# Encoder layer with dense expert products: where the transposes of two gate builds stand among blocks of U, and where the first G is loaded

## The chip, the cores and the metric

The kernel runs on one core of a Trainium2 chip. The metric is the device time of one execution in microseconds (us), lower is better. The engines are TensorE (PE; PEld is its weight load), VectorE (DVE), ScalarE (ACT), GpSimd (POOL) and SyncE (SP). SP, ACT and POOL also issue DMA transfers; rows of SPq or ACTq are such issues.

## What is computed

One post-norm encoder layer on 512 tokens of width 1024: layer norm, a combined in-projection, neighbourhood attention and latent attention, an output projection, a layer norm, then a mixture of 16384 experts with one row of U and one of V each, a gate, and the last layer norm. The experts are what the change touches:

```python
def one_chunk(xb):                                  # 128 tokens
    q = (xb @ w_q).reshape(128, 8, 256)
    s1 = jnp.einsum('thd,kd->thk', q[..., :128], sub_keys[0])
    s2 = jnp.einsum('thd,kd->thk', q[..., 128:], sub_keys[1])
    v1, i1 = lax.top_k(s1, 16)
    v2, i2 = lax.top_k(s2, 16)
    ...
    cv, ci = lax.top_k(cand, 16)                    # 16 of 256 sums
    e1 = jnp.take_along_axis(i1, ci // 16, axis=-1)
    e2 = jnp.take_along_axis(i2, ci % 16, axis=-1)
    idx = (e1 * 128 + e2).reshape(128, 8 * 16)      # 128 experts a token
    g = jax.nn.softmax(cv, axis=-1).reshape(128, -1)
    hpre = jnp.einsum('td,ted->te', xb, u_table[idx])
    act = g * jax.nn.gelu(hpre, approximate=False)
    return jnp.einsum('te,ted->td', act, v_table[idx])
```

## The kernel before

The 512 tokens are four chunks of 128. For chunk 0 the rows of U and V that its tokens chose are gathered. Chunk 1 (`NGC`) takes its U products from gathered rows ("own rows") and V densely. Chunks 2 and 3 are dense in both: all 16384 rows of U are multiplied, and a matrix G, mostly zeros, holds each token's gate weight for each expert. The gates make the dense result equal to the sparse one.

**The blocks of U.** U comes in blocks of 512 KB (tile `raw` or `raw_u`), loaded by SP (L1251) as buffers come free. `lead_block` multiplies a block with the 256 dense tokens (`whole`) in eight products of 128x256 (L1291) into a PSUM tile, "mm" or, in the stage `gating` at the end, one of two "hp" buffers. ACT applies the Gelu (`ge`, L1273); the first 96 results are sent to `ge_dram` on ACT's queue (L1275). 108 blocks (LEAD) are multiplied ahead of the loop. `run_pe(amount)` hands out products of U one by one until an account, `due`, is used up: so the written order on each engine is fixed when the program is built, and a constant such as `LAG` or `WAIT` is an amount of U products to put at a place.

**A build of G** (`build_g`) begins with three transposes on PE (L1090: the two expert indices and the weights, `e1`, `e2`, `gw`). DVE and ACT cast them out of PSUM (`eT` and `ne`, L1098, L1101, L1102, L1103, L1104). Then come 16 sets: DVE and ACT write one-hot rows (`oh_i`, L1144, L1148, L1149; `oh_j`, L1156), PE multiplies 16 pairs of them (L1115, into two PSUM tiles "tr"), and ACT copies the result to `g_st` (L1128). After four sets a quarter of G is complete and is sent to `g_dram` in four parts on ACT's queue (L1073); `send` issues one part, and `run` calls it once per step. The builds are those of chunk 2, chunk 3 ("the second build") and chunk 1 ("the last build").

**Rows.** POOL gathers one row of U per token (L1174) into five buffers in turn (`whi`, `wlo`, `row`, `whi`, `wlo`), DVE takes its product with the token (L1176, into `s_dot` for own rows, `hdot` for chunk 0). The own rows go beside the second build, 26 rows of chunk 0 (`beside`) beside the last. Near the end of these, at row 14 of 26, `SEAM` puts a lot of U products off, so that two sets of the last build follow each other with none between.

**The loop's first G.** The loop over 128 expert blocks that follows (L1551, `acc`; V blocks as `v_raw`, L1489) reads G in groups of eight blocks (tile `gt`, L1474). The first group, `first_g`, is loaded from `g_dram` early (L1447), but the quarters of chunk 1 are copied into it from `g_st`.

**Where the order is set.** All this stands in one written order for the five engines. What the words below call "ahead of" is a place in that order on one engine; semaphores make the engines wait for each other. Each DMA issue of SP and ACT takes the next of eight completion semaphores in turn, and so waits for the DMA eight issues back.

Of the kernel before, what the change touches and what calls it, by code (L numbers as in the profile page):

```python
# [31 lines left out]
N_S = 128  # L32
N_U = N_D - N_S
GT = 32
G_PARTS = 4
GB = 8
LEAD = 108
SPILL = 96
# [2 lines left out]
FIRST = 40  # L41
PACE = 1.1
AHEAD = 14.0
LAG = 6.0
BESIDE = 26
PRE = BESIDE
OWN = 1.2
OWN_G = 0.7
OWN_G_LATE = 4.0
SEAM = 7.0  # L50
WAIT = 8.4
OWN_LATE = 10.0
LATE = 0.57
OT = 8
# [25 lines left out]
def tile_encoder_layer(ctx: ExitStack, tc: tile.TileContext, A: dict, out: bass.AP):  # L80
    nc = tc.nc
# [214 lines left out]
    with tc.tile_pool(name="ln0", bufs=1, reuse_waits="tile") as ln0, \  # L296
# [122 lines left out]
        parts = turn(0)  # L419
# [17 lines left out]
        parts = turn(1)  # L437
# [8 lines left out]
        parts = turn(2)  # L446
# [8 lines left out]
        parts = turn(3)  # L455
# [374 lines left out]
    NGC, NDC = N_G // 128, N_D // 128  # L830
# [3 lines left out]
    g_dram = dram.tile([NTG, 128, 128 * GT], F32, name="g_dram")  # L834
# [107 lines left out]
    for g in range(16):  # L942
# [8 lines left out]
        if g:  # L951
            i, t = next(homes)
# [113 lines left out]
    parts = []  # L1066

    def send():

        if parts:  # L1070
            g, t, x = parts.pop(0)
            n = 128 // G_PARTS
            nc.scalar.dma_start(g_dram[g][:, x * n * GT:(x + 1) * n * GT],  # L1073
                                t[:, x * n:(x + 1) * n].rearrange("p i t -> p (i t)"))

    def run_pe(amount):
        nonlocal due
        due += amount * PACE
        while due > 0:
            done = next(pe_work, 1e9)  # L1080
            due -= done
        if due < -1e6:
            due = 0.0

    def build_g(c, e1, e2, gw):
# [55 lines left out]
        for q in range(128 // OT):  # L1141
            oh = bt.tile(wide, F16, name="oh_i")
            by_v = [128, 2 * np_ - OI_ACT, 128, 2]
            nc.vector.tensor_tensor(oh[:, OI_ACT:], pairs.unsqueeze(1).to_broadcast(by_v),  # L1144
                                    keys[:, q].rearrange("p s (a b) -> p (s a) b", b=2)[:, OI_ACT:].unsqueeze(2)
                                    .to_broadcast(by_v), op=OP.is_equal)
            for i in range(2 * OI_ACT):
                nc.scalar.activation(oh[:, i // 2, :, i % 2], iota, AF.Abs, bias=ne[:, OT * q + i:OT * q + i + 1])  # L1148
            nc.scalar.activation(oh[:, 0:OI_ACT], oh[:, 0:OI_ACT], AF.Relu, bias=1.0, scale=-1.0)  # L1149
            if ahead:  # L1150
                sums = products(*ahead)
                due -= G_SPLIT
            yield SPLIT_OH
            oj = bt.tile([128, 2, np_, 128, 2], F16, name="oh_j")
            for part in range(2):
                nc.vector.tensor_tensor(oj[:, part], oh[:, np_:],  # L1156
                                        wt[:, q, part].rearrange("p (a b) -> p a b", b=2).unsqueeze(2)
                                        .to_broadcast([128, np_, 128, 2]), op=OP.mult)
                if part == 0:
                    yield SPLIT_OJ  # L1160
            if ahead:
                leave(ahead[0], sums)
            ahead = (q, oh, oj)
            yield SPLIT_OJ
# [93 lines left out]
    def fill():  # L1258
        while loaded < LEAD and load_u():
            pass  # L1260
# [158 lines left out]
    with tc.manual_schedule(engines={nc.vector.engine, nc.scalar.engine, nc.tensor.engine, nc.sync.engine,  # L1419
                                     nc.gpsimd.engine}):  # L1420
        fill()
        held = []
        run(route(NGC, held))
        own = own_rows(*held)
        run_pe(next(own))
        own_due = -OWN_LATE
        for c in range(NGC + 1, 4):
            res = []
            if c > NGC + 1:
                run(route(0, []), OWN)  # L1430
            run(route(c, res), OWN)
            if c > NGC + 1:
                run_pe(WAIT)
            run(build_g(c, *res), OWN)
        own_due = 1e9
        run([0.0], 1.0)
        side = beside()
        run_pe(next(side))
        for _ in own:
            pass  # L1440
        own = None
        run_pe(LAG)

        while parts:
            send()
        first_g = pX.tile([128, NTG, GB, GT], F32, name="gt1")
        nc.sync.dma_start(first_g[:, 128 // GT:].rearrange("p g i t -> p g (i t)"),  # L1447
                          g_dram[128 // GT:, :, SPILL * GT:(SPILL + GB) * GT].rearrange("g p x -> p g x"))
        build = build_g(NGC, *held)
        next(build)  # L1450
        run_pe(next(side))
        own = side
        own_due = -OWN_G_LATE
        run(build, OWN_G)
        for x in own:
            run_pe(x)
        while parts:
            send()
        pb.close()
# [103 lines left out]
    with tc.manual_schedule(engines={nc.vector.engine, nc.sync.engine}):  # L1563
        for n, i in enumerate(order):
# [38 lines left out]
            parts = [t.rearrange("p (g t) -> p g t", t=GT) for t in (ah, al)] + [a]  # L1603
            if n in v_cut:
                held_a.append([t[:, :N_S // GT] for t in parts])
                parts = [t[:, N_S // GT:] for t in parts]
# [131 lines left out]
```

## Time and profile before

| | |
|---|---|
| time, median of 3 runs | 1490.76 us (1490.73 to 1491.14) |
| the profiled execution | 1489.54 us, span 1487.8 us |
| the second and the last build with the U blocks beside them | about 700 to 893 us |
| second build's transposes, last build's transposes | just ahead of DVE's casts at 712.32 and 810.35 us |
| last gate product, end of U, start of the loop | 878.27, 893.29, 893.29 us |
| the loop over expert blocks | 893 to about 1440 us |

All times in rows are microseconds from the start of the span. A row of the timeline has start, duration, engine, line, operation, out<-in, the shape, the count, and in brackets the idle time ahead of it with what released it. A row of a view of windows has the window, its length, the busy time of PE, PEld, DVE, ACT and POOL, the granted clock of TensorE (1.00 is full speed), the mean busy share of the DMA engines and GB/s. A row of the waits has the engine and line that waited, the one that it waited for, us in total, times, and the longest.

### The profile page before, as it was taken

Reading aid. Unit: us, or ns where it says so; the run is one execution under the profiler, and the core shown is the slowest. Engines: PE = TensorE matmul, PEld = TensorE weight load, DVE = VectorE, ACT = ScalarE, POOL = GpSimd, SP = SyncE. Lnnn points to the kernel's source line nnn. Section 1 sums busy time; section 2 is a strip of 40 time slices with the busy share of each in tenths; the row PEclk is TensorE's granted clock in tenths of the full one; section 3 lists DMA queues with packets and bytes.
Section 4 is the critical chain, followed back from the end, with each engine's and each line's share of the span. In section 5 each row is a group of like instructions: output and inputs, shape, how many; then the busy total and the mean of one; then the engine's idle time right before and its main releaser. Section 6 shows DMA issues by size and latency. Waiting matters only on the chain.

```text
span 1487.8 us, 22518 instructions
## 1 busy us (share of the span) xinstructions
PE 1450.2 (97%) x7693; PEld 1212.4 (81%) x7693; DVE 1268.5 (85%) x2736; ACT 638.4 (43%) x1203; POOL 570.7 (38%) x520
## 2 busy tenths in 40 slices
PE   9999999999999999999998999999999999999997
PEld 5788777788888878888887888988888888888775
DVE  7376786579998979998776987999899999999997
ACT  3355776243221554212555763444343333333433
POOL 1013110010014544344442435665555666666630
PEclk9999999999999999999999999999999999999999
DMA  7333340175239999999999999999999999999992
GB/s 255 99 111 92 97 128 30 29 245 170 100 125 351 334 416 415 405 324 336 392 416 410 376 396 369 415 417 417 401 393 411 412 412 411 412 412 412 411 362 85
DMA packets 196851, 453.82 MB, mean 305 GB/s; under 512 B 18945, under 2 KB 96897, under 8 KB 196738
## 3 DMA queue, kind: packets, MB, share of 16 engines
q1 hardware_dynamic: 119168, 211.72, 38.6%
q0 software_dynamic: 57984, 207.12, 35.5%
q10 hardware_dynamic: 19586, 33.57, 5.9%
q8 instruction: 60, 0.98, 0.2%
q14 instruction: 53, 0.43, 0.1%
HBM read 411.70 MB, written 37.75 MB: 302 GB/s over the span
## 4 chain that ended last, share of the span: by engine, by line
PE 56%; DMA 22%; DVE 9%; issue 6%; ACT 4%; POOL 3%; SPq 0%; ACTq 0%; DVEq 0%; POOLq 0%
PE acc L1551 16%; DMA raw<-in_v_rows_dram 11%; PE mm L1291 6%; PE hp L1291 5%; DMA ge_dram<-ge 4%; PE mm L129 4%; PE mm L131 4%; PE mm L130 4%; PE pj L129 3%; PE pj L130 3%; PE pj L131 3%; DMA v_raw<-in_v_rows_dram 3%; PE hp L129 1%; PE hp L131 1%; PE hp L130 1%
## 5 line engine op out<-in xcount | busy, mean ns | idle before, releaser
L110 DVE TENSOR_TENSOR wlo<-raw,whi 128x1024 fp32r<-128x1024 f32 (+4 forms) x113 | 131.5, 1164 | 45.7 <-ACT whi L110 45.4
L110 ACT CAST a_hi<-gt 128x384 fp32r<-128x384 f32 (+2 forms) x128 | 64.9, 509 | 242.4 <-DVE gt L1598 179.5
L110 ACT CAST whi<-raw 128x1024 fp32r<-128x1024 f32 (+4 forms) x113 | 113.0, 1001 | 106.9 <-PE mm L130 47.3
L1291 PE MATMUL mm<-whole,raw 128*128 128x256 f32 x672 | 153.1, 381 | 1.5 <-DMA raw<-in_uT_dram 1.5
L1174 POOL DMA_INDIRECT whi<-in_u_rows_dram,s_ix x51 | 64.2, 1259 | 218.5 <-DVE cand L994 129.7
L1551 PE MATMUL acc<-hTh,a_hi 128*128 128x512 f32 x456 | 141.8, 391 | 0.1
L1551 PE MATMUL acc<-hTl,a_hi 128*128 128x512 f32 x456 | 141.2, 390 | 0.0
L1551 PE MATMUL acc<-hTh,a_lo 128*128 128x512 f32 x456 | 140.9, 389 | 0.0
L1291 PEld LDWEIGHTS mm<-whole,raw 128*128 128x128 f32 x672 | 125.6, 190 | 17.9 <-DMA raw<-in_uT_dram 1.9
L1534 POOL DMA_INDIRECT gat<-in_v_rows_dram,i_sel x64 | 100.8, 1574 | 55.0 <-DVE base L1536 39.5
L110 ACT CAST hTh<-v_raw 128x1024 fp32r<-128x1024 f32 x74 | 77.8, 1051 | 55.9 <-PE acc L1551 23.1
L1551 PEld LDWEIGHTS acc<-hTl,a_hi 128*128 128x128 f32 x456 | 85.4, 188 | 18.3 <-DVE hTl L110 0.4
L1551 PEld LDWEIGHTS acc<-hTh,a_lo 128*128 128x128 f32 x456 | 85.4, 188 | 18.2 <-DVE a_lo L110 0.3
L1551 PEld LDWEIGHTS acc<-hTh,a_hi 128*128 128x128 f32 x456 | 84.1, 188 | 17.2 <-ACT a_hi L110 1.1
L110 DVE TENSOR_TENSOR hTl<-v_raw,hTh 128x1024 fp32r<-128x1024 f32 x74 | 90.2, 1219 | 6.4 <-ACT hTh L110 6.4
L1551 PE MATMUL acc<-wlo,a_hi 128*128 128x512 f32 x300 | 92.8, 390 | 0.2
L1551 PE MATMUL acc<-whi,a_hi 128*128 128x512 f32 x300 | 92.8, 391 | 0.1
L1551 PE MATMUL acc<-whi,a_lo 128*128 128x512 f32 x300 | 92.6, 390 | 0.0
L1174 POOL DMA_INDIRECT wlo<-in_u_rows_dram,s_ix x51 | 61.9, 1213 | 68.3 <-DVE s_dot L1176 56.0
L1519 POOL DMA_INDIRECT gat<-in_u_rows_dram,i_sel x52 | 69.1, 1329 | 45.2 <-DVE hdot L1525 34.1
L1536 DVE SCALAR_TENSOR_TENSOR base<-gat,hdot,base 128x1024 f32<-128x1024 f32 x64 | 82.0, 1281 | 1.0
L1273 ACT ACTIVATE ge<-mm 128x256 f32<-128x256 f32 x78 | 29.6, 380 | 110.4 <-PE mm L1291 100.5
(415 smaller groups left out, 3815.7 us busy)
## 6 DMA issues: line engine op xcount, KB each, us to landing
raw<-in_uT_dram SPq DMA_DIRECT2D x80, 512.0 KB, 7.8
v_raw<-in_v_rows_dram SPq DMA_DIRECT2D x78, 512.0 KB, 13.2
raw<-in_v_rows_dram SPq DMA_DIRECT2D x48, 512.0 KB, 13.8
g_dram<-g_st ACTq DMA_DIRECT2D x40, 512.0 KB, 12.1
ge_dram<-ge ACTq DMA_DIRECT2D x96, 128.0 KB, 7.0
ge<-ge_dram SPq DMA_DIRECT2D x96, 128.0 KB, 13.0
gt<-g_dram SPq DMA_DIRECT2D x30, 384.0 KB, 13.9
raw_u<-in_uT_dram SPq DMA_DIRECT2D x19, 512.0 KB, 7.8
```

What stands on the lines that cost most here:

```text
L110: cut = nc.scalar.copy(hi, src), nc.vector.tensor_tensor(lo, src, r32(hi), op=OP.subtract)
L129: nc.tensor.matmul(ps, a[0], b[0], start=start, stop=False)
L130: nc.tensor.matmul(ps, a[0], b[1], start=False, stop=False)
L131: nc.tensor.matmul(ps, a[1], b[0], start=False, stop=stop)
L1174: nc.gpsimd.indirect_dma_start(out=u[:], out_offset=None, in_=u_rows, in_offset=bass.IndirectOffsetOnAxis(ap=ix[:, k:k + 1], axis=0))
L1273: nc.scalar.activation(ge, ps[:, :N_U], AF.Gelu)
L1291: nc.tensor.matmul(ps[:, :N_U], raw[:, k], whole[:, k, :], start=(k == 0), stop=(k == 7))
L1519: nc.gpsimd.indirect_dma_start(out=u[:], out_offset=None, in_=u_rows, in_offset=bass.IndirectOffsetOnAxis(ap=i_sel[:, c, k:k + 1], axis=0))
L1534: nc.gpsimd.indirect_dma_start(out=u[:], out_offset=None, in_=v_rows, in_offset=bass.IndirectOffsetOnAxis(ap=i_sel[:, c, k:k + 1], axis=0))
L1536: nc.vector.scalar_tensor_tensor(base[c], u, hdot[:, c, k:k + 1], base[c], op0=OP.mult, op1=OP.add)
L1551: nc.tensor.matmul(acc[c][hf], a[:, cs], b[:, hf * 512:(hf + 1) * 512], start=(n == 0 and i == 0), stop=(n == 127 and i == 2))
```

## The change

Four things move, and no arithmetic changes:

- `WAIT` 8.4 becomes 3.0: fewer products of U between the routing of chunk 3 and the transposes of the second build. 14 products go from ahead of them to behind them.
- `LAG` 6.0 becomes 1.0: fewer products of U ahead of the last build's transposes. Before, 17 products stood between the second build's last gate products and the transposes, and 11 between these and the first gate product; now 4 and 19.
- `GAP_ROWS`: four rows of `beside` instead of one stand between the last transposes and their casts (with the one ahead of them, DVE does five rows ahead of `eT` instead of two).
- `load_first()`: the remaining sends of chunk 3 and the load of `first_g` go from ahead of the last build's transposes into its set 6 (`FIRST_G_AT`). The sends that stood together are now spread, one per step.

Because the account is kept, the products that leave these places turn up later: behind the last gate product there stood 33, and now 50. Between the sets the numbers are nearly the same (last build before 6, 7, 6, 10, 6, 7, 9, 6, 10, 2, none, 4, 7, 6, 9; now 7, 6, 7, 9, 7, 6, 10, 1, none, 5, 6, 10, 6, 7, 9). POOL's order is unchanged. Line numbers move by 2 to 11: L1090 becomes L1099, L1115 L1124, L1251 L1262, L1291 L1302, L1447 L1082, L1073 L1075, L1273 L1284, L1101 L1110, L1176 L1187, L1489 L1497, L110 L112.

```diff
--- before.py
+++ after.py
@@ -41,14 +41,16 @@
 FIRST = 40
 PACE = 1.1
 AHEAD = 14.0
-LAG = 6.0
+LAG = 1.0
 BESIDE = 26
 PRE = BESIDE
 OWN = 1.2
 OWN_G = 0.7
 OWN_G_LATE = 4.0
 SEAM = 7.0
-WAIT = 8.4
+WAIT = 3.0
+FIRST_G_AT = 6
+GAP_ROWS = 4
 OWN_LATE = 10.0
 LATE = 0.57
 OT = 8
@@ -1073,6 +1075,13 @@
             nc.scalar.dma_start(g_dram[g][:, x * n * GT:(x + 1) * n * GT],
                                 t[:, x * n:(x + 1) * n].rearrange("p i t -> p (i t)"))
 
+    def load_first():
+
+        while parts and parts[0][0] >= N_S // GT:
+            send()
+        nc.sync.dma_start(first_g[:, N_S // GT:].rearrange("p g i t -> p g (i t)"),
+                          g_dram[N_S // GT:, :, SPILL * GT:(SPILL + GB) * GT].rearrange("g p x -> p g x"))
+
     def run_pe(amount):
         nonlocal due
         due += amount * PACE
@@ -1147,6 +1156,8 @@
             for i in range(2 * OI_ACT):
                 nc.scalar.activation(oh[:, i // 2, :, i % 2], iota, AF.Abs, bias=ne[:, OT * q + i:OT * q + i + 1])
             nc.scalar.activation(oh[:, 0:OI_ACT], oh[:, 0:OI_ACT], AF.Relu, bias=1.0, scale=-1.0)
+            if c == NGC and q == FIRST_G_AT:
+                load_first()
             if ahead:
                 sums = products(*ahead)
                 due -= G_SPLIT
@@ -1441,14 +1452,11 @@
         own = None
         run_pe(LAG)
 
-        while parts:
-            send()
         first_g = pX.tile([128, NTG, GB, GT], F32, name="gt1")
-        nc.sync.dma_start(first_g[:, 128 // GT:].rearrange("p g i t -> p g (i t)"),
-                          g_dram[128 // GT:, :, SPILL * GT:(SPILL + GB) * GT].rearrange("g p x -> p g x"))
         build = build_g(NGC, *held)
         next(build)
-        run_pe(next(side))
+        for _ in range(GAP_ROWS):
+            run_pe(next(side))
         own = side
         own_due = -OWN_G_LATE
         run(build, OWN_G)
```

The start of the last build on PE, before (`e1s`, `e2s` and `gws` are the operands of its transposes, LDWEIGHTS and the product behind it the first gate product):

```order
L1291 MATMUL mm<-whole,raw_u 128x256 x4
L1291 MATMUL mm<-whole,raw 128x256 x13
L1090 MATMUL tr<-ident,e1s 128x128
L1090 MATMUL tr<-ident,e2s 128x128
L1090 MATMUL tr<-ident,gws 128x128
L1291 MATMUL mm<-whole,raw 128x256 x11
L1115 LDWEIGHTS oh_j
L1115 MATMUL tr<-oh_i,oh_j 128x128
```

The same place now:

```order
L1302 MATMUL mm<-whole,raw 128x256 x4
L1099 MATMUL tr<-ident,e1s 128x128
L1099 MATMUL tr<-ident,e2s 128x128
L1099 MATMUL tr<-ident,gws 128x128
L1302 MATMUL mm<-whole,raw 128x256 x5
L1302 MATMUL mm<-whole,raw_u 128x256 x8
L1302 MATMUL mm<-whole,raw 128x256 x6
L1124 LDWEIGHTS oh_j
L1124 MATMUL tr<-oh_i,oh_j 128x128
```

Thirteen products that stood ahead of the transposes are no longer there, and eight more stand behind them, ahead of the first gate product.

The same place on ACT, before (`g_st` and `ge` are copies out of PSUM, `eT` the casts of the transposes):

```order
L1273 ACTIVATE ge<-mm 128x256
L1275 DMA ge_dram<-ge 128x256
L1128 ACTIVATE g_st<-tr 128x128x4 x2
L1073 DMA g_dram<-g_st 128x1024
L1273 ACTIVATE ge<-mm 128x256
L1275 DMA ge_dram<-ge 128x256
L1273 ACTIVATE ge<-mm 128x256
L1275 DMA ge_dram<-ge 128x256
L1073 DMA g_dram<-g_st 128x1024 x3
L1101 ACTIVATE eT<-tr 128x16x8
L1102 ACTIVATE eT<-tr 128x128
L1148 ACTIVATE oh_i<-iota,eT 128x128 x4
```

And now:

```order
L1137 ACTIVATE g_st<-tr 128x128x4 x4
L1075 DMA g_dram<-g_st 128x1024
L1284 ACTIVATE ge<-mm 128x256
L1286 DMA ge_dram<-ge 128x256
L1284 ACTIVATE ge<-mm 128x256
L1286 DMA ge_dram<-ge 128x256
L1110 ACTIVATE eT<-tr 128x16x8
L1111 ACTIVATE eT<-tr 128x128
L1075 DMA g_dram<-g_st 128x1024
L1157 ACTIVATE oh_i<-iota,eT 128x128 x4
L1158 ACTIVATE oh_i<-oh_i 128x512
L1075 DMA g_dram<-g_st 128x1024 x2
```

The three sends that stood together ahead of `eT` are spread: one directly behind it, two behind the first `oh_i`.

SP's queue around the load of the first G (`gt` with a number is that tile, `raw` and `raw_u` blocks of U, `gb` a block of V), before:

```order
L1251 DMA raw<-in_uT_dram 128x1024 x3
L1251 DMA raw_u<-in_uT_dram 128x1024
L1251 DMA raw<-in_uT_dram 128x1024
L1447 DMA gt_7619<-g_dram 128x8x256
L1251 DMA raw<-in_uT_dram 128x1024 x2
L1251 DMA raw_u<-in_uT_dram 128x1024
L1251 DMA raw<-in_uT_dram 128x1024 x3
```

And now, the rows counted from the same place:

```order
L1262 DMA raw<-in_uT_dram 128x1024 x3
L1262 DMA raw_u<-in_uT_dram 128x1024
L1262 DMA raw<-in_uT_dram 128x1024 x3
L1262 DMA raw_u<-in_uT_dram 128x1024
L1262 DMA raw<-in_uT_dram 128x1024
L1082 DMA gt_7569<-g_dram 128x8x256
L1262 DMA raw<-in_uT_dram 128x1024 x2
L1226 DMA gb<-in_v_rows_dram 128x1024
```

The load stands four loads of U further back.

The end of ACT's work ahead of the loop (`whi<-v_raw` casts the first V block that needs it, `hTh` and `a_hi` are other casts for the loop), before:

```order
L1273 ACTIVATE ge<-mm 128x256 x2
L110 CAST hTh<-h_s 128x1024
L110 CAST a_hi<-gt_7619 128x256
L1473 COPY gt_8567<-g_st 128x256 x2
L1273 ACTIVATE ge<-mm 128x256
L110 CAST a_hi<-gt_7619 128x256
L110 CAST a_hi<-gt_7619 128x128 x2
L110 CAST whi<-v_raw 128x1024
L1273 ACTIVATE ge<-hp 128x256 x2
L110 CAST a_hi<-gt_7619 128x384
```

And now:

```order
L112 CAST hTh<-h_s 128x1024
L1284 ACTIVATE ge<-mm 128x256 x2
L1284 ACTIVATE ge<-hp 128x256 x2
L112 CAST a_hi<-gt_7569 128x256
L1481 COPY gt_8567<-g_st 128x256 x2
L112 CAST a_hi<-gt_7569 128x256
L112 CAST a_hi<-gt_7569 128x128 x2
L112 CAST whi<-v_raw 128x1024
L1284 ACTIVATE ge<-hp 128x256 x3
```

Five blocks instead of two end in "hp" buffers, and three of their `ge` instead of two stand behind the cast of `v_raw`.

## The prediction

> **What bounds the kernel now.** I read the page first, then the busy time of each engine by stage, then the waits of the stage that the change touches, and last the timeline around its two places. The page's engine rows name TensorE:
>
> ```profile
> PE 1450.2 (97%) x7693; PEld 1212.4 (81%) x7693; DVE 1268.5 (85%) x2736; ACT 638.4 (43%) x1203; POOL 570.7 (38%) x520
> ```
>
> A share over the whole span doesn't say where time can be had, so here are the stretch that the change rewrites (700 to 893 us) and the loop over expert blocks behind it. The columns are busy us of PE, PEld, DVE, ACT and POOL, then the granted clock, the DMA share and GB/s.
>
> ```profile
> 700.00:893.00 193.00, 184.14 (x1212) 161.37 (x1211) 150.34 (x245) 115.40 (x285) 74.12 (x63) 0.99 1.01 398
> 893.00:1440.00 547.00, 546.67 (x2629) 459.58 (x2629) 519.75 (x698) 213.63 (x306) 333.03 (x226) 1.00 1.03 408
> ```
>
> In the loop PE idles 547.00 − 546.67 = 0.33 us, so nothing can be won there. It can only start earlier. What holds it is PE alone, as two rows show: the first cast that the loop needs on ACT waited for PE's products, and POOL's next gathers sat behind the end of U.
>
> ```profile
> 900.12 0.51 ACT L110 CAST a_hi<-gt 128x384 fp32r<-128x384 f32 x1 [6.05 <-PE acc L1551]
> 894.41 0.94 POOL L1519 DMA_INDIRECT gat_w<-in_u_rows_dram,i_sel  x1 [14.14 <-issue]
> ```
>
> So the end follows the moment at which PE is through with U, and that moment is PE's work (unchanged in number) plus PE's idle time before it. That idle time is 193.00 − 184.14 = 8.86 us, and the waits of PE in this stretch (us in total, times, longest) account for it:
>
> ```profile
> PE tr L1115 <- ACT g_st L1128: 5.1, 5, 1.7
> PE mm L1291 <- DMA raw<-in_uT_dram: 1.5, 1, 1.5
> PE tr L1115 <- DVE oh_j L1156: 1.2, 2, 0.9
> PE tr L1115 <- ACT oh_i L1149: 1.1, 1, 1.1
> ```
>
> VectorE waits too, 14.1 us for the two sets of transposes, but that is idle time off the path unless PE then waits for what DVE began late:
>
> ```profile
> DVE eT L1098 <- PE tr L1090: 14.1, 2, 8.2
> DVE whi L1176 <- DMA whi<-in_u_rows_dram,s_ix: 6.9, 6, 1.7
> ```
>
> The ceiling of any gain is thus 8.86 us plus what a low clock cost. DMA sets another: 193 us at 398 GB/s is 76.8 MB, and at the loop's 408 GB/s they take 188.3 us, 4.7 less. It can be exceeded only as far as the engines move more.
>
> **The price of one U product.** All moves are counted in products of a U block (eight to a block, two records each in the trace):
>
> ```profile
> 883.12 3.62 PE L1291 MATMUL mm<-whole,raw 128*128 128x256 f32 x16
> 886.58 7.07 PE L1291 MATMUL hp<-whole,raw 128*128 128x256 f32 x32
> 893.29 0.81 PE L1551 MATMUL acc<-hTh,a_hi 128*128 128x512 f32 x2
> ```
>
> From 883.12 to 886.58 one block passes: 3.46 us, 0.433 us a product.
>
> **Second build: transposes 14 products earlier.** By the order 14 products of U move from ahead of the transposes to behind them: 14 × 0.433 = 6.06 us. The number between transposes and first gate product stays 26, so PE comes to every gate product of this build 6.06 us earlier. DVE's first cast waited 5.90 us:
>
> ```profile
> 712.32 0.42 DVE L1098 CAST eT<-tr 128x256 f16<-128x256 f32 x1 [5.90 <-PE tr L1090]
> ```
>
> It therefore starts 5.90 earlier, not 6.06. Both engines move as a pair, and what PE waits for in this build stays: 0.9 us of the oh_j waits (1.2 less the 0.30 below) and 5.1 − 1.11 − 1.72 = 2.3 us of the g_st waits. Cost: 0.16 us, at most the longest landing of a row, 1.7; I take 0.2.
>
> **Last build: transposes earlier, four rows ahead.** Before, these rows stood there:
>
> ```profile
> 802.08 0.08 DVE L1176 DVE_READ_ACCUMULATOR2_ANT hdot<- 128x1 f32 x1
> 810.35 0.42 DVE L1098 CAST eT<-tr 128x256 f16<-128x256 f32 x1 [8.18 <-PE tr L1090]
> 811.29 2.24 ACTq L1073 DMA_DIRECT2D g_dram<-g_st  x3
> 813.58 0.28 ACT L1101 ACTIVATE eT<-tr 128x128 f16<-128x128 f32 x1 [5.41 <-DMA ge_dram<-ge]
> 814.06 0.29 DVE L1104 SCALAR_TENSOR_TENSOR eT<-tr,eT 128x128 f16<-128x128 f32 x1 [3.09 <-ACT eT L1102]
> 816.08 0.22 PE L1115 MATMUL tr<-oh_i,oh_j 128*128 128x128 f16 x1 [1.09 <-ACT oh_i L1149]
> 816.60 1.03 PE L1115 MATMUL tr<-oh_i,oh_j 128*128 128x128 f16 x15 [0.30 <-DVE oh_j L1156]
> ```
>
> ACT reached its part of eT only at 813.58, behind three sends of G that took 2.24 us to issue and had waited. DVE lost 3.09 us on that, and PE 1.09 + 0.30 = 1.39. After, the transposes are 26 products (11.3 us) earlier, the first gate product 18 products (7.8 us): PE wants it at 816.08 − 1.09 − 7.8 = 807.2. ACT has one send in front of eT instead of the block of three, spread one to a step. DVE must first do five rows where it did two. Its part before them is done 5.9 earlier, so two rows end at 796.3 (802.16 − 5.9). The other three wait for their gathers: they were issued at
>
> ```profile
> 794.78 1.17 POOL L1174 DMA_INDIRECT whi<-in_u_rows_dram,i_sel  x1 [0.30 <-issue]
> 796.25 1.03 POOL L1174 DMA_INDIRECT wlo<-in_u_rows_dram,i_sel  x1 [0.30 <-issue]
> whi<-in_u_rows_dram,i_sel POOLq DMA_INDIRECT x1, 10.7
> wlo<-in_u_rows_dram,i_sel POOLq DMA_INDIRECT x1, 11.1
> ```
>
> and the last number of the DMA rows (stretch 788 to 798) is the median landing in us. Released by DVE, they go out 5.9 earlier: the last lands at 796.25 − 5.9 + 11.1 = 801.5, its row ends 1.2 later at 802.7, and DVE begins the casts. From there to the first product it needed 816.08 − 810.35 − 3.09 = 2.6 us: 805.3, against 807.2. Slack is 1.9 us, so the 1.39 us go. Lower bound of this term: the gaps come back in full size (gain 0), or PE waits 2.1 us, 0.7 more than now, if the last gather takes 4 us longer than measured. I take 1.39, since the measured landings fit.
>
> **The load of the first G goes to set 6 of the last build.** Its place on SP's queue was
>
> ```profile
> 819.76 0.38 SPq L1447 DMA_DIRECT2D gt<-g_dram  x1
> 820.23 1.07 SPq L1251 DMA_DIRECT2D raw<-in_uT_dram  x2
> 827.99 1.35 PE L1291 MATMUL mm<-whole,raw 128*128 128x256 f32 x5 [1.46 <-DMA raw<-in_uT_dram]
> 815.00:825.00 10.00, 8.62 (x74) 7.65 (x75) 9.90 (x15) 8.69 (x24) 2.57 (x2) 1.00 0.75 260
> ```
>
> It was issued only at 819.76, once the last sends of G had landed; two loads of U stood behind it, DMA fell to a share of 0.75, and one late block cost PE 1.46 us. In the new order the load stands four U loads later, and its sends were issued some six sets before. It then waits for nothing, so 1.46 us go. Its 1 MB takes 2.5 us of DMA at 408 GB/s, against a U load that is used blocks later. Bounds: gain 0 (a landing gap moves to another block) to 1.46; I take 1.46.
>
> **The seam and its clock.** Two sets stand on PE without U between them:
>
> ```profile
> 859.04 1.11 PE L1115 MATMUL tr<-oh_i,oh_j 128*128 128x128 f16 x16 [1.11 <-ACT g_st L1128]
> 861.87 1.86 PE L1115 MATMUL tr<-oh_i,oh_j 128*128 128x128 f16 x16 [1.72 <-ACT g_st L1128]
> 860.00:862.00 2.00, 0.28 (x5) 0.16 (x3) 2.00 (x3) 1.97 (x6) 0.65 (x1) 0.80 1.02 416
> 862.00:863.00 1.00, 1.00 (x11) 1.00 (x10) 1.00 (x4) 1.00 (x4) 0.28 (x1) 0.50 1.03 418
> ```
>
> Idle 1.11 + 1.72 us, and then the granted clock falls to 0.50; the stretch of 860 to 864 costs about 1 us of speed. The new order keeps a pair of sets without U (one product ahead of it instead of two), and the wait is for ACT, whose work in a set is the same. Change taken 0, from −1 (a product less of cover, 0.43, and sends of G now issued there) to +3.8. [...]
>
> **The tail.** The 17 products (7.4 us) that leave the front stand behind the last gate product. The number of blocks that end in the two "hp" buffers grows from two to five; the fifth needs ACT's ge of the third, and on ACT's queue that now stands behind the cast of the first V block:
>
> ```profile
> 879.86 0.33 SPq L1251 DMA_DIRECT2D raw<-in_uT_dram  x1
> 880.54 1.52 SPq L1489 DMA_DIRECT2D v_raw<-in_v_rows_dram  x3
> 890.92 1.05 ACT L110 CAST whi<-v_raw 128x1024 fp32r<-128x1024 f32 x1 [2.18 <-DMA v_raw<-in_v_rows_dram]
> 891.87 0.38 ACT L1273 ACTIVATE ge<-hp 128x256 f32<-128x256 f32 x1
> gat<-in_u_rows_dram,i_sel POOLq DMA_INDIRECT x4, 9.2
> ```
>
> V's load is issued behind U's last load, both before and after 893.29 − 880.54 = 12.75 us ahead of U's end; the fifth block must start 3.46 ahead of it, the cast and ge take 1.05 + 0.38. A landing of up to 12.75 − 3.46 − 1.43 = 7.9 us costs nothing, the 10.4 measured (890.92 − 880.54) costs 2.5. Those 10.4 were shared with the four gathers of the last row (issued between 866 and 881, 9.2 us to landing). They follow the rows of the last build on POOL's queue, and so come some 7 us earlier against U's end. Without them I expect a landing in the lower half of what V's first loads show (870 to 920 us; min, median, max):
>
> ```profile
> DMA to landing us min/median/max: 3.8/7.3/11.6
> ```
>
> Taken 0; range 0 to 5.4 (page's median for all V loads, 13.2, worked as above: 13.2 − 7.9 = 5.3).
>
> **The sum.** −1.39 − 1.46 + 0.2 + 0 + 0 = −2.65 us, made against the profiled execution: 1489.54 (span 1487.8 and 1.74 around it), 1.22 under the median of 1490.76. The median should become 1488.1. A measurement tells no difference of under about 0.2% (2.98 us) from no change, so this stands just inside that.
>
> **Rivals.**
> - *More goes.* The waits for g_st at the seam and at the second build's end shrink as well: up to 1.11 + 1.72 + 1 more at the seam. Then 2.65 + 3.83 = 6.5 us, 1484.3. For it: DVE has three rows fewer to put beside the sets, and DMA has idle room only where SP was blocked. Against it: the waits are for ACT, and DMA's ceiling of about 4.7. Chance 0.24.
> - *It doesn't do what it says.* DVE and ACT come late to the casts (landings of 13 instead of 11 use up the 1.9 us of slack, or a send holds ACT again), and the two gaps are as long as before, or one grows by what the other loses: 1490.7. For it: ACT has a send and two ge transfers directly ahead of eT. Chance 0.17.
> - *Slower.* The fifth "hp" block waits for V's first load. It eats the gain from a landing of 7.9 + 2.65 = 10.6 us, and decides by more than 0.2% from 7.9 + 2.65 + 2.98 = 13.5, near the page's median for V loads; at 14 the time is 1490.76 + 6.1 − 2.65 = 1494.2. Against it: the 3.8 to 11.6 of the first loads. Chance 0.08.
>
> **How the numbers follow.** The forecast has 0.51, on both sides of the 0.2% line: its own range is 1486 (part of the seam goes) to 1490 (V lands at 10.4), 0.22 of it faster by over 0.2% and 0.29 within. Faster: 0.22 + 0.24 = 0.46; same: 0.29 + 0.17 = 0.46; slower 0.08. The range of 1483.5 to 1491.5 takes in both gains and the case without one, and leaves out the slow case, the ends of that without one and the fullest gain, about 0.2.
>
> **What would show it.** After: the two waits of eT for transposes shrink to under 1 us; the three G sends no longer stand together; no "raw" wait near the last build's start; SP's wait for g_dram gone; first gate product of the last build near 807; U ends near 890.6. Wrong: a wait of "hp" for ACT ge behind 880, a first product later than 809 with DVE's casts behind a row, or seam gaps over 4 us with more slices at clock 0.50.

## The result, and the profile after

The changed kernel takes 1500.77 us (median of 6 runs, 1499.93 to 1505.33) against 1490.68 us before (6 runs): a ratio of 1.0075, 95% interval 1.0061 to 1.0088. The forecast was 1488.1 with a range up to 1491.5, so the change went the other way, by 10 us.

First the stretch up to the loop and the loop itself (columns as before the change):

```profile
700.00:904.00 204.00, 185.46 (x1216) 162.87 (x1215) 151.97 (x245) 116.45 (x286) 76.08 (x63) 0.97 0.98 382
904.00:1440.00 536.00, 535.77 (x2581) 450.41 (x2580) 511.13 (x686) 208.96 (x302) 337.08 (x225) 1.00 1.03 406
```

The loop still has no idle PE time (0.23 us), so the 10 us lie ahead of it: PE idles 18.5 us there instead of 8.9. Its waits in 700 to 904 us are down to two kinds, and one is large:

```profile
PE tr L1124 <- ACT g_st L1137: 15.0, 4, 10.5
PE tr L1124 <- DVE oh_j L1167: 3.5, 2, 2.1
```

The timeline of PE gives the places (start, duration, the idle time ahead of it in brackets), with the last gate product and the start of the loop:

```profile
816.29 1.11 PE L1124 MATMUL tr<-oh_i,oh_j 128*128 128x128 f16 x16 [3.39 <-ACT g_st L1137]
854.61 1.86 PE L1124 MATMUL tr<-oh_i,oh_j 128*128 128x128 f16 x16 [10.49 <-ACT g_st L1137]
881.02 1.08 PE L1124 MATMUL tr<-oh_i,oh_j 128*128 128x128 f16 x16
903.39 0.81 PE L1559 MATMUL acc<-hTh,a_hi 128*128 128x512 f32 x2
```

The last gate product begins 2.75 us later than before (878.27), although it was to come earlier, and the 17 further products of U behind it take 17 x 0.433 = 7.4 us. The sum, 10.1, is the shift of the loop's start (893.29 to 903.39).

PE's releaser at both places is ACT, and ACT itself stood. These are its two rows, the load of the first G on SP, and that load's landing (last number, us) before and after:

```profile
813.77 1.31 ACT L1157 ACTIVATE oh_i<-iota,eT 128x128 f16<-128x128 f32 x4 [4.94 <-DMA ge_dram<-ge]
851.64 1.31 ACT L1157 ACTIVATE oh_i<-iota,eT 128x128 f16<-128x128 f32 x4 [7.82 <-DMA gt<-g_dram]
832.54 0.64 SPq L1082 DMA_DIRECT2D gt<-g_dram  x1
```

```profile
gt<-g_dram SPq DMA_DIRECT2D x1, 1024.0 KB, 5.6
gt<-g_dram SPq DMA_DIRECT2D x1, 1024.0 KB, 18.7
```

No ACT instruction reads the parts of `gt` that this load writes at that time. ACT waits for it because the send of G ahead of `oh_i` in its queue is the eighth DMA issue behind the load (load, ge, send, U, ge, ge, U, V, send), and takes the same completion semaphore (number 110 for both in the trace). The load was issued at 832.54 and landed 18.7 us later, at 851.2; the send was issued at 851.26. Before the change, the load landed in 5.6 us.

The load of before fell into a stretch with room on DMA (815 to 825 us, share 0.75), the load of after did not (share 1.04 from its issue at 832.54 to its landing at 851.24). Here are 740 to 860 us of the kernel before and of the one after, the 20 us behind that of the one after, and then the stretch from the last gate product to the loop, of each:

```profile
740.00:860.00 120.00, 112.86 (x792) 98.46 (x790) 93.16 (x150) 75.81 (x189) 43.82 (x37) 1.00 1.01 402
740.00:860.00 120.00, 101.46 (x703) 88.61 (x702) 93.78 (x151) 72.99 (x181) 46.05 (x38) 0.96 1.03 409
860.00:880.00 20.00, 20.00 (x151) 17.80 (x149) 14.85 (x23) 16.10 (x38) 8.32 (x7) 1.00 0.95 342
878.27:893.29 15.02, 15.02 (x83) 13.34 (x82) 11.15 (x19) 7.47 (x16) 1.70 (x2) 1.00 1.02 385
881.02:903.39 22.37, 22.37 (x117) 19.81 (x116) 8.85 (x16) 7.30 (x17) 0.00 (x0) 1.00 0.71 233
```

From 740 to 860 DMA is full (share 1.03), and with the change PE is busy 11 us less in that time. From 860 on it is the other way round: PE has no idle time up to the loop, and DMA falls to 342 and then 233 GB/s. The change took the work of the two apart.

### The profile page after: what moved, and what is told of

The parts are those of the page before. It is cut to its first block, busy times and chain, and to the rows that moved or that the text cites. A ratio compares the mean times of both kernels' runs of the same rounds, so it can differ in the third digit from the quotient of the medians.

```text
span 1498.6 us, 22521 instructions
## 1 busy us (share of the span) xinstructions
PE 1452.5 (97%) x7693; PEld 1212.2 (81%) x7693; DVE 1270.5 (85%) x2736; ACT 639.0 (43%) x1203; POOL 576.9 (38%) x520
## 4 chain that ended last, share of the span: by engine, by line
PE 50%; DMA 15%; DVE 13%; issue 11%; POOL 7%; ACT 3%; ACTq 0%; POOLq 0%; SPq 0%; DVEq 0%
PE acc L1559 19%; DMA ge<-ge_dram 6%; PE mm L131 3%; PE mm L132 3%; PE mm L133 3%; PE pj L131 3%; POOL wlo L1185 3%; POOL whi L1185 3%; PE pj L132 3%; PE pj L133 3%; DMA whi<-in_u_rows_dram,s_ix 3%; DMA gt<-g_dram 2%; PE mm L1302 2%; PE hp L1302 2%; DMA raw<-in_v_rows_dram 2%
## 5 line engine op out<-in xcount | busy, mean ns | idle before, releaser
L112 ACT CAST a_hi<-gt 128x384 fp32r<-128x384 f32 (+2 forms) x128 | 64.9, 508 | 252.4 <-DVE gt L1606 188.1
L112 DVE TENSOR_TENSOR wlo<-raw,whi 128x1024 fp32r<-128x1024 f32 (+4 forms) x113 | 131.5, 1165 | 44.5 <-ACT whi L112 44.2
L112 ACT CAST whi<-raw 128x1024 fp32r<-128x1024 f32 (+4 forms) x113 | 113.0, 1001 | 101.1 <-PE mm L132 41.2
L1302 PE MATMUL mm<-whole,raw 128*128 128x256 f32 x640 | 147.2, 381 | 0.0
L1302 PEld LDWEIGHTS mm<-whole,raw 128*128 128x128 f32 x640 | 118.9, 190 | 14.8
L1559 PEld LDWEIGHTS acc<-hTl,a_hi 128*128 128x128 f32 x456 | 85.3, 188 | 18.5 <-DVE hTl L112 0.7
L112 ACT CAST hTh<-v_raw 128x1024 fp32r<-128x1024 f32 x74 | 77.7, 1050 | 50.9 <-PE acc L1559 23.4
L112 DVE TENSOR_TENSOR hTl<-v_raw,hTh 128x1024 fp32r<-128x1024 f32 x74 | 90.3, 1220 | 6.7 <-ACT hTh L112 6.7
L112 DVE TENSOR_TENSOR a_lo<-gt,a_hi 128x384 fp32r<-128x384 f32 (+2 forms) x128 | 69.7, 546 | 21.4 <-ACT a_hi L112 21.1
```

Of the source, the lines that this page charges most:

```text
L112: cut = nc.scalar.copy(hi, src), nc.vector.tensor_tensor(lo, src, r32(hi), op=OP.subtract)
L1302: nc.tensor.matmul(ps[:, :N_U], raw[:, k], whole[:, k, :], start=(k == 0), stop=(k == 7))
L1559: nc.tensor.matmul(acc[c][hf], a[:, cs], b[:, hf * 512:(hf + 1) * 512], start=(n == 0 and i == 0), stop=(n == 127 and i == 2))
```

## The experiments

Five theories stand in the expectations. A: the load of the first G holds ACT through the shared semaphore, and that is all. B: its transfer crowds the others. C: the earlier order as such brings the gate products ahead of ACT and DVE. D: DMA is full and sets when the build ends. E, formed from the first eight: D, and long landings turn into stalls of ACT or SP through the semaphores and the order of the queues. The line numbers of rows shift by a few between kernels.

All runs in one table: U products behind the last gate product (from the written order), start of that product's group and end of U in the profile, and the median with the ratio to the kernel before, which was measured again beside each group of runs (medians 1490.68 for after, 1489.29 for e1 to e4, 1490.46 for e5 to e8, 1490.30 for e9 to e12, 1490.00 for e13 to e15). Between groups the ratios are the safer comparison.

| run | products behind | last gate product | end of U | median us | ratio (95%) |
|---|---|---|---|---|---|
| before | 33 | 878.27 | 893.29 | 1490.68 | |
| after | 50 | 881.02 | 903.39 | 1500.77 | 1.0075 (1.0061 to 1.0088) |
| e1 load back | 50 | 880.86 | 903.22 | 1501.10 | 1.0093 (1.0073 to 1.0112) |
| e2 load alone | 33 | 881.25 | 896.28 | 1493.59 | 1.0031 (1.0015 to 1.0046) |
| e3 load in set 9 | 50 | 875.89 | 898.26 | 1500.14 | 1.0071 (1.0047 to 1.0095) |
| e4 load on GpSimd | 50 | 880.67 | 903.04 | 1497.26 | 1.0059 (1.0037 to 1.0080) |
| e5 SEAM 0 | 34 | 886.19 | 901.65 | 1500.49 | 1.0076 (1.0057 to 1.0095) |
| e6 LAG and WAIT alone | 59 | 882.14 | 908.39 | 1501.19 | 1.0069 (1.0048 to 1.0089) |
| e7 four rows alone | 24 | 885.95 | 897.09 | 1496.59 | 1.0048 (1.0030 to 1.0066) |
| e8 before, SEAM 3.5 | 24 | 879.77 | 890.92 | 1487.74 | 0.9987 (0.9974 to 1.0001) |
| e9 after, half the rows | 50 | 873.04 | 895.41 | 1491.39 | 1.0015 (1.0002 to 1.0029) |
| e10 before, half the rows | 33 | 877.89 | 892.92 | 1485.99 | 0.9976 (0.9966 to 0.9985) |
| e11 after, GpSimd and SEAM 0 | 34 | 879.62 | 895.08 | 1492.09 | 1.0017 (1.0000 to 1.0033) |
| e12 before, GpSimd and SEAM 3.5 | 24 | 878.10 | 889.24 | 1486.19 | 0.9972 (0.9962 to 0.9982) |
| e13 before, load on GpSimd | 33 | 879.06 | 894.08 | 1488.86 | 0.9995 (0.9984 to 1.0006) |
| e14 e13 and LAG 1 | 45 | 876.93 | 897.14 | 1494.20 | 1.0035 (1.0020 to 1.0050) |
| e15 e13 and WAIT 3 | 46 | 878.07 | 898.71 | 1498.02 | 1.0049 (1.0035 to 1.0064) |

In every row the end of U is the last gate product plus 0.92 plus 0.433 a product, to within 0.25 us, and the span ends 592.5 to 595.2 us behind it. So two columns hold the whole story: when the last gate product comes, and how much U stands behind it. The profiles don't reach this stretch at the same moment: the first build's transposes, which no run moves, begin at 479.8 to 483.8 us, and the second build's at 709.2 to 715.1 with `WAIT` 8.4 and at 703.7 to 707.3 with `WAIT` 3. A difference of a few us between two last gate products can be older than the stretch. The profiled run isn't always at the median (e3's runs go from 1492.7 to 1502.9 and its profile is of one at 1494.2; e6's profile is of its slowest, 1505.4, e10's of one at 1490.1).

**e1, the load and the sends back in their place.**

```diff
-            if c == NGC and q == FIRST_G_AT:
-                load_first()
...
+        while parts:
+            send()
         first_g = pX.tile([128, NTG, GB, GT], F32, name="gt1")
+        load_first()
         build = build_g(NGC, *held)
```

> The change with the first G's load and the sends ahead of it put back ahead of the last build's transposes; LAG 1, WAIT 3 and GAP_ROWS 4 stay. Theory A (ring): the load of 1 MB takes 18.7 us to land, and the send of G on ACT that is the eighth DMA issue behind it reuses its completion semaphore, so ACT stands 7.8 us at the seam and PE 10.5 us; with the load out of there the seam's wait falls back to about 3 us and the time to 1489 to 1493. Theory B (contention): the load's small pieces slow the other transfers around 835 to 855; it predicts the same here. Theory C (the earlier transposes and the four rows bring the seam ahead of ACT and DVE): the seam still costs 8 us or more, time 1499 to 1502.

The seam's wait did fall, to 2.64 us, as A had it, and nothing was won. Another stall took its place (PE's timeline, and SP's issue of the load):

```profile
824.71 2.93 PE L1300 MATMUL mm<-whole,raw 128*128 128x256 f32 x6 [9.71 <-DMA raw<-in_uT_dram]
813.95 0.38 SPq L1082 DMA_DIRECT2D gt<-g_dram  x1
```

SP's issue ahead of it was at 798.94, the load 15.0 us later. The waits of e6 and e7, where the load stands at the same place, name the sends of G (SP's L1082 waited 13.6 and 14.5 us for `g_dram<-g_st` to land). The U loads queued behind it, from 814.42 on, and PE ran out of U for 9.71 us. A alone is refuted, B with it (it expected the same here), and so is C in its simple form: its time came true, but the seam isn't what costs here.

**e2, the load's move alone** (`LAG = 6.0`, `WAIT = 8.4`, `GAP_ROWS = 1`, else as after).

> The kernel before with the load's move alone (set 6), LAG 6, WAIT 8.4, one row. A: here the eighth issue behind the load is the second send of that quarter, issued some 17 us behind it, so ACT is held by 0 to 4 us and PE by less than in the whole change; the late U load (1.5 us) goes: 1488 to 1494. B: seam of 8 us or more as in the whole change, 1496 to 1501. C: nothing lost, 1489 to 1490.

0.3% slower, at the upper end of A's range. The load holds ACT here too, 7.2 us where A had at most 4, and instead of the U block at 828 us one at 853 is late:

```profile
ACT g_raw L1284 <- DMA gt<-g_dram: 7.2, 1, 7.2
853.10 2.93 PE L1302 MATMUL mm<-whole,raw_u 128*128 128x256 f32 x6 [4.46 <-DMA raw_u<-in_uT_dram]
```

**e3, the load in set 9** (`FIRST_G_AT = 9`).

> The whole change with the load in set 9 instead of 6, so that it is issued behind the sends of that quarter and the eighth issue behind it is a load of V on SP's queue (h_s), not a send on ACT. A: ACT isn't held by the load, seam about 3 us, 1490 to 1494, and SP's load of h_s waits for the load of G instead. B: the transfer collides with the next ones, 1496 or more. C: 1499 or more.

A missed: the median stays at 1500, which the ranges of B and C hold. Its runs spread over 10 us; in the quick one that was profiled, neither SP nor ACT waits for the load from 740 to 880 us, but ACT still stands for a ge send (4.8 us) and for landings of G (3.7 us ahead of `g_st`, 2.3 ahead of `oh_i`), PE at the seam for 4.96.

**e4, the load on GpSimd's queue** (`nc.gpsimd.dma_start` in `load_first`).

> The whole change with the load in the same set 6 but issued on GpSimd's queue, whose transfers use other completion semaphores: same bytes, same place, no reuse by ACT. A: the wait of ACT for the load goes, seam about 3 us, 1490 to 1494 (unless the issue itself holds up GpSimd's row gathers, which would show as DVE waits for rows). B: the seam stays at 8 us or more, 1498 or more. C: the same as B.

By the medians 3.5 us were won of the 10, by the ratios 2.4 (1.0075 to 1.0059, and the intervals overlap): less than A had it. ACT waits for the load no more, but PE still waits 11.6 us for ACT:

```profile
PE tr L1124 <- ACT g_st L1137: 11.6, 6, 4.0
ACT g_st L1137 <- DMA g_dram<-g_st: 5.7, 4, 2.1
ACT oh_i L1157 <- DMA ge_dram<-ge: 5.1, 1, 5.1
```

The last gate product stands at 880.67 without the hold and at 881.02 with it: this, with e1, gave theory D. What went is ACT's wait for the load. In the traces of before and after the issues of SP and ACT carry eight completion semaphores between them (numbers from 100 to 110) and those of GpSimd eight others (111 to 118). ACT still waits 5.7 and 5.1 us for the landings of its own transfers, and no row here shows which DMA engines carried the load. The run isn't quite the same place either: on GpSimd's queue the load was issued at 825.25, not 832.54, after a wait of 10.03 us that also held the row gathers behind it; DVE's waits for these rows rose from 3.1 to 5.5 us.

**e5, the whole change with SEAM 0** (`SEAM = 0.0`).

> The whole change with SEAM 0 instead of 7: the 16 U products that the seam puts off stand between the sets there, so 34 instead of 50 stand behind the last gate product (33 in the kernel before). Theory D (new, from the windows of the first four): from 740 us to the last gate product DMA is at its most (share 1.03, 414 to 417 GB/s) and sets when the builds end, 878 to 881 us whatever PE does; products put behind them are added to the end at 0.433 us each while DMA runs at 233 GB/s. It predicts a last gate product at 880 to 884, U's end near 896, time 1491 to 1495. Theory A (ACT held by the load at the seam): ACT is still held 7 us, PE has 16 products to do meanwhile, but what is won there is lost nowhere: also 1492 to 1495, with a last product not later than now. Theory C (the earlier order as such): 1499 to 1502.

A miss for D and for A: 16 products fewer behind, and 1500 all the same, which only C's range holds. The last gate product slid to 886.19 (D: 880 to 884), and now an SP load waited 12.6 us on the semaphore of the load of G, and a U block behind it came 5.97 us late:

```profile
SPq L1226 <- DMA gt<-g_dram: 12.6, 1, 12.6
856.20 1.22 PE L1302 MATMUL mm<-whole,raw 128*128 128x256 f32 x2 [5.97 <-DMA raw<-in_uT_dram]
```

**e6, LAG 1 and WAIT 3 alone, and e7, four rows alone** (both on e1, the other constants as before).

> The kernel before with LAG 1 and WAIT 3 alone (load and sends where they were, one row): 59 products behind the last gate product. D: the last one still at 877 to 881, so the end of U is 59 x 0.433 = 25.5 us behind it, 903 to 907, time 1500 to 1505, the worst of all. A: no load in the build, ACT isn't held: 1488 to 1492. C: 1496 to 1500.

> The kernel before with GAP_ROWS 4 alone: four rows ahead of the last casts, 20 products there instead of 11, and 24 behind the last gate product instead of 33. D: fewer products behind, so not slower unless the last gate product itself comes later; as the build starts 4 us later on PE, the last product comes at 881 to 884 and U's end at 891.5 to 895: 1488 to 1493. A: 1490 to 1491, nothing of it touches the load. C (the rows are what costs): 1494 or more.

e6 is as slow as e1, within D's range at its low end, and refutes A; in its profile, of its slowest run, the last gate product and the end of U lie 1.1 and 1.4 us behind D's. e7 is slower than D had it, its last gate product 2 us later than D's latest, and only C's bound holds it. Both stall on U blocks behind the load, as e1 does:

```profile
827.01 1.22 PE L1300 MATMUL mm<-whole,raw 128*128 128x256 f32 x2 [9.44 <-DMA raw<-in_uT_dram]
829.31 4.79 PE L1300 MATMUL mm<-whole,raw 128*128 128x256 f32 x12 [6.07 <-DMA raw<-in_uT_dram]
```

**e8, the kernel before with SEAM 3.5** (`SEAM = 3.5`).

> The kernel before with SEAM 3.5 instead of 7: 9 products go from behind the last gate product to the two sets of the seam, where PE idles 2.8 us and then runs 1 us slow: 24 behind. D: the gate products are paced by DMA, so the products put between them are nearly free as far as PE idles there: U's end up to 3.9 us earlier, 1487 to 1490. If PE paced the builds already: 1490 to 1491. A slower time (1494 or more) would say that the first V blocks come too late behind a shorter tail.

1487.74, by 0.13% and just inside the noise, as D had it: nine products fewer behind, and the last gate product 1.5 us later.

**e9 and e10, half the rows, on after and on before.** Both leave out 13 of the 26 row gathers, so what they compute lacks the products of those rows.

```diff
+            few = len(ks) == BESIDE
+            j = k // 2 if few else k
+            if not (few and k % 2):
-            u = (...).tile([128, D], F32, name=("whi", "wlo", "row", "whi", "wlo")[k % 5], ...)
-            nc.gpsimd.indirect_dma_start(...)
+                u = (...).tile([128, D], F32, name=("whi", "wlo", "row", "whi", "wlo")[j % 5], ...)
+                nc.gpsimd.indirect_dma_start(...)
```

> The whole change, with every second of chunk 0's 26 rows beside the last build not gathered (DVE takes the row before once more, so those 13 products are of the wrong row): 13 x 512 KB = 6.8 MB less on DMA between 780 and 880 us, PE's, DVE's and ACT's work and order unchanged. Theory E (DMA is full from 740 us on, so transfers land late; the eight shared completion semaphores and the order of the queues turn that into stalls of ACT or SP, and the end of the build stays where the transfers put it): with room on DMA the stalls of 3.4 and 10.5 us shrink to 3 us or less in all, the last gate product comes at 868 to 873 and the time falls to 1485 to 1492, what was predicted for the change. A (the load of the first G alone holds ACT through its semaphore): that load is as large as before, so at least 5 us of the seam's wait stay, 1494 to 1499. C (the earlier order as such): 1499 or more.

> The same 13 gathers left out of the kernel before. E: before has little to win, since PE's own work bounds it up to its 8.9 us idle: 1483 to 1489, and the change on top of it (the run beside this one) makes no more than 3 us difference to either side. A and C: 1488 to 1490, and the change stays 5 us or more slower than this.

With 6.8 MB less on DMA, and the same load on the same semaphore, the changed kernel falls by 9.4 us to 1491.39. The load lands some 12.4 us after its issue instead of 18.7 (issued at 830.50, ACT's held send let go at 842.93). ACT's hold for it shrinks from 7.8 to 1.5 us, the seam's wait to 4.15, and the last gate product comes 8 us earlier, of which 2.2 were there at the second build's transposes (703.66 against 705.85):

```profile
ACT oh_i L1157 <- DMA gt<-g_dram: 1.5, 1, 1.5
846.22 1.86 PE L1124 MATMUL tr<-oh_i,oh_j 128*128 128x128 f16 x16 [4.15 <-ACT g_st L1137]
873.04 1.08 PE L1124 MATMUL tr<-oh_i,oh_j 128*128 128x128 f16 x16
```

The kernel before gains 4.7 by the same cut. So the change costs 10.1 us with all the rows and 5.4 with half of them: about half of its cost goes with the traffic, and half doesn't. E had the difference at 3 us at most; there A and C, with 5 or more, were right, though neither had the times of e9 and e10. Waits of 7.3 us for ACT (3.18 at 812 and the 4.15) stay in the changed kernel. The cut isn't of traffic alone: DVE's waits for these rows (3.1 us in after) go with it.

**e11, after with both undone** (e4 and e5 together).

> The whole change with two things undone at once: the first G's load on GpSimd's queue (no shared semaphore) and SEAM 0 (34 instead of 50 products behind the last gate product). Each alone left 1497 and 1500: the first still had 50 products behind, the second had SP stand 12.6 us for the load. E: with neither, the last gate product comes at 879 to 884 and U ends 14.7 us later: 1489 to 1494. If a third stall takes their place (a late U block, ACT at a send): 1495 or more.

1492.09, as E had it (its runs go from 1488.7 to 1499.3). Each alone had won 3.5 and 0.3 us, both together 8.7.

**e13 to e15: one transposition at a time, without the load's stalls** (the kernel before with the load of e4; then `LAG = 1.0`; or `WAIT = 3.0`).

> The kernel before with the first G's load in set 6 on GpSimd's queue and nothing else: 33 products behind the last gate product, as before. E: the late U block goes and ACT isn't held by the load: 1487 to 1490, and the rest of what e12 won comes from SEAM 3.5. It is the base for the next two.

> The same with LAG 1 as well: the last build's transposes 13 products earlier, 45 products behind its last gate product instead of 33. E: DMA is full, so the last gate product comes no more than 1 us earlier and the 12 products are added behind it (5.2 us): 1491 to 1496. If PE paced the build, the products would only change places: 1487 to 1490.

> The same base with WAIT 3 instead of LAG 1: the second build's transposes 14 products earlier, 46 products behind the last gate product. E: the second build too runs with DMA full from 740 us on, so again the last gate product stays and 13 products (5.6 us) come behind: 1491 to 1496. If PE paced the second build: 1487 to 1490.

The base is level with the kernel before. LAG costs 5.3 us on it at the median. In the profile, the end of U is 3.1 us later: 12 products more behind (5.2) and a last gate product 2.1 earlier, more than E's 1. The earlier build meets a stall of the same kind without the load: PE waits at the seam for ACT, and ACT for a ge send (5.6 us):

```profile
853.51 1.87 PE L1124 MATMUL tr<-oh_i,oh_j 128*128 128x128 f16 x16 [5.04 <-ACT g_st L1137]
```

WAIT costs 9.2, more than E had; its runs lie in two groups, 1493.4 to 1494.4 and 1498.0 to 1498.6. The profile is of the first, with 13 products more (5.6) and a last gate product 1.0 earlier. What the second group adds wasn't seen in a profile and stays open.

**e12, a version that beats both** (the kernel before with `SEAM = 3.5` and the load in set 6 on GpSimd's queue).

> A version that might beat both: the kernel before (LAG 6, WAIT 8.4, one row) with SEAM 3.5 and the first G's load in set 6 of the last build on GpSimd's queue. It should lose the late U block (1.3 us) and the three sends ahead of eT, and keep what SEAM 3.5 won: E: 1484 to 1488. If the load's issue holds up the row gathers behind it on GpSimd's queue: 1488 to 1493.

1486.19, 0.28% below the kernel before (0.18 to 0.38%). 24 products behind, the last gate product at 878.10, no late U block, and the seam has one wait:

```profile
PE tr L1124 <- ACT g_st L1137: 3.9, 5, 2.8
856.44 1.26 PE L1124 MATMUL tr<-oh_i,oh_j 128*128 128x128 f16 x16 [2.80 <-ACT g_st L1137]
```

## Why the prediction was wrong, step by step

The prediction counted PE's idle time ahead of the end of U, and so the traces can be set against it term by term. PE's idle time ahead of each place, in us:

| place | before | after | change predicted | change measured |
|---|---|---|---|---|
| second build | 3.2 | 4.5 | +0.2 | +1.4 |
| start of the last build | 1.4 | 3.4 | −1.4 | +2.0 |
| late U block behind the load | 1.5 | 0 | −1.5 | −1.5 |
| seam | 2.8 | 10.5 | 0 | +7.7 |

The changes add up to +9.6 against the −2.65 of the forecast; the loop starts 10.1 us later, and the remaining 0.5 is about what the longer half speed (below) adds. The step that failed is the seam, put at no change. Smaller misses are the start of the last build, where PE waits for ACT, and the second build, where it waits for DVE.

- *The loop follows the end of U.* Right: the span ends 594.5 us behind it before and 595.2 after.
- *Second build: both engines move as a pair, 6.06 us earlier, cost 0.2.* This step failed first, by a small amount. Its transposes came 5.9 earlier, but the last gate product of the build only 4.2 (801.41 to 797.18): 1.8 lost, not 0.2. PE waited 3.5 us for DVE's `oh_j` there instead of 0.9:

```profile
801.41 1.11 PE L1115 MATMUL tr<-oh_i,oh_j 128*128 128x128 f16 x16 [0.37 <-ACT g_st L1128]
797.18 1.11 PE L1124 MATMUL tr<-oh_i,oh_j 128*128 128x128 f16 x16 [0.84 <-ACT g_st L1137]
781.11 1.04 PE L1124 MATMUL tr<-oh_i,oh_j 128*128 128x128 f16 x15 [2.10 <-DVE oh_j L1167]
```

  That the pair moved while the row gathers, sends and loads that feed it could not, with DMA full from 740 us on (share 1.03 from 740 to 800), fits this but isn't shown.
- *Last build: gaps of 1.39 go.* Right at the place: DVE's cast at 805.31 (802.7 predicted) and a first gate product at 808.44 without a wait (807.2). But the next group waited 3.39 for ACT, which stood 4.94 for a ge send's semaphore. That was named in the rival without gain ("a send holds ACT again") and priced too low.

```profile
805.31 0.42 DVE L1107 CAST eT<-tr 128x256 f16<-128x256 f32 x1
808.44 1.38 PE L1124 MATMUL tr<-oh_i,oh_j 128*128 128x128 f16 x16
```

- *The load waits for nothing, so 1.46 go.* The late U block went, and the load waited for nothing. The step asked what the load waits for, and not who waits for the load: the eighth issue behind it. It also took its cost as bandwidth (2.5 us) and not as a landing, 18.7. Without the hold (e4) most of the loss stays, so this is one stall among several and not the whole cause.
- *Seam: change 0, from −1 to +3.8.* It was +7.7 (10.49 against 1.11 + 1.72), outside that range, for the cause just named. The prediction had named a gap of over 4 us there as a sign of being wrong, but no rival gave it a price. The clock followed:

```profile
844.00:854.00 10.00, 0.12 (x3) 0.10 (x1) 6.59 (x11) 1.99 (x6) 3.72 (x3) 0.73 1.04 414
854.00:858.00 4.00, 3.40 (x20) 3.11 (x20) 1.42 (x2) 3.56 (x9) 0.00 (x0) 0.50 1.02 418
```

  Behind the gap the granted clock stood at 0.50 for 4 us, which costs some 2 us, against about 1 before, where it stood at 0.50 for 2 us (862 to 864).
- *Tail: 0.* The stall that was feared didn't come: the cast of the first V block ran without a wait and the five "hp" blocks follow without a gap. The 17 products in it cost nothing by themselves, since PE must run them somewhere. But the forecast needed the last gate product to come earlier by as much (7.4 us) and more, and it came 2.75 later, so they were added to the end.

```profile
895.63 1.04 ACT L112 CAST whi<-v_raw 128x1024 fp32r<-128x1024 f32 x1
```

- *DMA's ceiling of 4.7 us.* The 2.65 forecast lay under it, so the sum didn't break it. But it was an average over 193 us. In windows of 20 us from 740 to 860, before, DMA moved 414, 416, 415, 377, 370 and 418 GB/s: nearly all the room lay between 800 and 840, around the hole at 815 to 825 which the load's move was to fill. The earlier transposes found none ahead of it.

So the slower side had a mechanism that was not among the rivals: the one named there (V's first load) did not occur. Shown are: the waits of the table above; the hold of ACT by the load (its row, 7.82 us, and e4 without it); that with less traffic the load lands sooner and holds ACT less (e9: 12.4 us against 18.7, and 1.5 against 7.8); that either move of the transposes costs 5 us or more with the load out of ACT's way (e14 5.3, e15 9.2, at the median); that products behind the last gate product are added to the end (the table of runs, 0.433 us each). That DMA sets when the last gate product comes is argued and not shown: it speaks for it that this product stays between 875.9 and 882.2 in fourteen of the seventeen orders, with 24 to 59 products behind it. Against it speak 886 in e5 and e7, a PE without idle time from 860 on, and the half of the cost that stays with half the rows. Why WAIT 3 costs two different amounts from run to run is not settled, nor why e7's median lies 3 us above the run that was profiled.

## What to carry to other kernels

Where PE and DMA are both nearly full (here from 740 to 860 us: PE busy 112.86 of 120 us, DMA's share 1.01), ask what ends the stage when PE has less to do there. Here PE's work that was moved out of the stretch left DMA's work in it as it was (PE busy 101.46 us, share 1.03). Take DMA's room from that stage alone. Filler that is put behind the stage's last result is paid in full unless that result comes earlier by as much: here 17 products cost their 7.4 us, and the result came 2.75 us later. A DMA that lands late is a wait for whoever reuses its completion semaphore, on SP's queue (12.6 us in e5) or ACT's (7.8 us in the changed kernel): count forward from every long transfer (here eight issues) before it is moved.

## What the runs showed that was not expected

- The same 1 MB load took 5.6 us to land where DMA had room (share 0.75) and 18.7 us amid the sends (share 1.04). On GpSimd's queue it took 8.8 us in e13; whether the queue or the moment made that difference no run separates.
- A transfer on GpSimd's queue took ACT's 7.8 us of hold away, though not its waits for other landings (e4: 2.4 to 3.5 us won in all). On the kernel before the same move won nothing clear of noise (e13).
- The three runs of the kernel before that stood at the start agreed within 0.4 us (1490.73 to 1491.14), but later runs of it went from 1485.5 to 1494.6. e3 spread over 10 us and e11 over 11; e15's seven runs lie in two groups 4 us apart. Three runs that agree don't show how far a kernel spreads.
